# Attention heads' values in the second half of the rounded-token tiles, the samples' rows of w_out multiplied amid attention

## The chip, the cores and the metric

The kernel runs on one core of one Trainium2 chip. The time is the device time of one launch in microseconds, here the median over several executions. The engines of the core are TensorE (PE, with its weight loads counted apart as PEld), VectorE (DVE), ScalarE (ACT), GpSimd (POOL) and SyncE (SP), which issues most of the transfers between the chip's memory and the on-chip buffers.

## The reference

One inference step of a decoder of two layers: a gated-linear-attention layer, then a differential-attention layer, each followed by a squared-ReLU MLP and layer norms. There is one prompt of 1024 tokens (plus 16 meta tokens) and there are 8 running samples with one new token each; a sample's past is 4096 keys and values in a paged cache. What matters here is the second layer's attention and the product with its output matrix `w_out` (1024 x 1024):

```python
def diff_core(q, k, v, q_pos, k_pos, lam):
    s = jnp.einsum('bqhmd,bkhmd->bhmqk', q, k).astype(F32) * (DIFF_DH ** -0.5)
    s = jnp.where(k_pos[None, :] <= q_pos[:, None], s, -jnp.inf)
    p = jax.nn.softmax(s, axis=-1)
    a = p[:, :, 0] - lam * p[:, :, 1]
    return jnp.einsum('bhqk,bkhe->bqhe', a, v.astype(F32))

def diff_output(o, g_sub, lam_init, w_out, dtype):
    o = rms_norm(o, g_sub) * (1.0 - lam_init)
    return o.reshape(B, T, DIFF_HEADS * DIFF_DV).astype(dtype) @ w_out
```

There are 8 heads with keys and queries of 2 x 64 and values of 128 columns. Both the prompt's tokens and the 8 samples go through `diff_output` with the same `w_out`.

## The kernel before

**Products.** Everything is float32. A large product is made of three matmuls on rounded operands (`mm3`, lines 199 to 201): each operand is split into a rounded part "hi" and the rest "lo", and hi x hi, hi x lo and lo x hi are added up in PSUM (tile `mmt`). The tokens' rounded parts are `XH` and `XL`, two tiles each (one for 512 tokens, with room for 8 blocks of features of 516 columns). A weight matrix comes in units of 256 columns (`kunit`, lines 176 to 191): four loads of 256 KB into `raw` (two buffers), four casts on ACT into `whi` (L186), four subtractions on POOL into `wlo` (L187). The tiles `whi` and `wlo` have two buffers each, so two units can be on the chip.

**The stages around the change.** The second layer's projection `w_in` runs with 12 units up to about 1777 us. Then comes the prompt's attention, one head after the other, to about 2051 us; then the product with `w_out` (its first matmuls lie inside the last head, its last at about 2160 us); then the MLP, in which PE is busy throughout.

**Attention.** A head has eight steps of 128 queries. `prep` (L1087, L195, L196) transposes the head's keys and queries, loaded by `load_qk` into `rqk`, and splits them into hi and lo: 1040 + 1024 = 2064 columns in the tile of `XH` and `XL` that belongs to the head's parity. The next head is prepared during this one. `front` makes a step's scores: PE (L1186, tile `prt`), DVE masks and takes the maximum (L1188), ACT takes the exponential (L1190, tile `as`), DVE combines both maps (L1194). `back` transposes that (PE, L1207, tile `axt`), ACT copies it to SBUF (L1209, `aT`), and PE multiplies it with the head's values (L1212) into an accumulator, tile `smt`, which has two buffers during attention; four steps share one accumulator, and ACT reads it twice, for the copy to `Y` (L1262) and the squares (L1266). `load_v` brings the head's values, 512 KB, one head ahead, into a buffer of `whi` which is idle then. When four or eight steps of the last head are done, `o_norm` and `o_fm` (L1232, L1233, L1234) normalise and transpose the tokens into `XH` and `XL` for `w_out`, one block of 128 features after the other.

**w_out.** `w_out` goes through four units and two halves of the tokens: units 0 and 1 with the first half, the same two with the second half, then units 2 and 3. Each unit and half has two accumulators. The generator `samples` is entered after the fourth accumulator: the samples' attention result `oT` is normalised (L1334 to L1340, with a power on POOL, L1339), put into `zoT`, a tile with 32 columns for each of 8 feature blocks, and multiplied with the rows of `w_out` in `s_rows` (L519): 16 matmuls of 32 columns, four on the four column groups of the array for each pair of feature blocks. They read the raw rows of `w_out` again, sixteen loads of 256 KB into five buffers `rw` (L1320). `s_post` (from L522) adds the residual and normalises.

**What sets the order.** The program text gives priorities, and a scheduler that simulates a timeline fixes the order of instructions on each engine at build time. Each engine then takes its instructions in that order and stops at one whose inputs or buffers are not ready. All transfers issued by SP form one such order too.

## Time and profile before

| what | us |
|---|---|
| median of 3 runs | 2855.34 (2853.87 to 2857.34) |
| the profiled execution, its own time | 2854.81 |
| its span, first to last instruction | 2853.1 |
| mean granted TensorE clock | 0.989 of full |
| attention, about | 1778 to 2051 |
| w_out, its first to its last matmul | 2023.8 to 2154.1 |
| samples' 32-column matmuls in it | 2075.6 to 2102.5 |

How to read the rows that the prediction shows. A row of the timeline has start, duration, engine, line, operation, output and inputs with their shapes, a count of records, and in brackets the idle time of the engine before it with what ended it. One 32-column matmul of float32 operands leaves two records, a transpose or a matmul of `mm3` one. Matmuls are pipelined, so the duration of one (0.28 us for w_out's) is longer than the distance to the next. A row of the windows has, for a stretch of time, its length, the busy time of each engine with the number of instructions, the clock, the share of the DMA engines' time and GB/s. A row of waits has the engine, its instruction and the instruction it waited for, with the sum, the number of times and the longest.

### The profile page before, as it was taken

To read this page: it belongs to the slowest core of one execution; us is meant where nothing else is said; L and a number is where in the kernel's file an instruction comes from. 1 tells how busy PE (TensorE), PEld (TensorE's weight loads), DVE (VectorE), ACT (ScalarE), POOL (GpSimd) and SP (SyncE) were. 2 spreads that over 40 slices of the span, in tenths; PEclk is the share of its full clock that TensorE was granted. 3 is DMA by queue.
4 is the path that set the end of the run, shared out by engine and by line. 5 is a ranking of instruction groups with operands and counts; after the bars stand their busy time and mean duration, and the time that the engine had idled before them with its cause. 6 is when DMAs were issued, how large, how long until landed. Compare 5 with 4: busy or idle time off the path is not lost.

```text
span 2853.1 us, 52265 instructions
## 1 busy us (share of the span) xinstructions
PE 2741.4 (96%) x19849; PEld 2241.7 (79%) x19849; DVE 1950.0 (68%) x3046; ACT 1094.0 (38%) x2229; POOL 1112.0 (39%) x744
## 2 busy tenths in 40 slices
PE   8889999999999999999999999998999999999997
PEld 5666677997777777777799988777888889797985
DVE  2565454668888777777667731888538887878788
ACT  3233344242221321221242112777615546355553
POOL 1221212233343443434234321000326767777764
PEclk9899999999999999999999999999999999999998
DMA  7557741634798898988648994111334455554574
GB/s 255 176 174 260 266 171 39 233 103 154 264 338 308 308 353 300 359 293 322 255 161 321 355 375 133 39 53 49 113 105 89 112 129 116 135 123 115 129 190 89
DMA packets 271833, 560.71 MB, mean 197 GB/s; under 512 B 23559, under 2 KB 138829, under 8 KB 267485
## 3 DMA queue, kind: packets, MB, share of 16 engines
q1 hardware_dynamic: 252284, 520.66, 52.2%
q0 software_dynamic: 19296, 36.71, 7.8%
q8 instruction: 156, 2.56, 0.4%
q14 instruction: 97, 0.79, 0.1%
HBM read 531.16 MB, written 29.26 MB: 196 GB/s over the span
## 4 chain that ended last, share of the span: by engine, by line
PE 74%; DVE 8%; DMA 6%; issue 5%; ACT 4%; POOL 2%; SPq 0%; DVEq 0%; POOLq 0%; ACTq 0%
PE mmt L199 18%; PE mmt L200 17%; PE mmt L201 17%; PE smt L843 4%; PE axt L199 3%; PE axt L200 3%; PE axt L201 3%; ACT as L1190 2%; PE smt L1212 2%; PE prt L1186 1%; PE smt L519 1%; DVE pg L802 1%; DMA swt<-in_mlp_w 1%; PE axt L1207 1%; DMA pg<-in_cache_k 1%
## 5 line engine op out<-in xcount | busy, mean ns | idle before, releaser
L187 POOL TENSOR_TENSOR wlo<-raw,whi 128x512 fp32r<-128x512 f32 x256 | 369.4, 1456 | 770.7 <-ACT whi L186 714.7
L199 PE MATMUL mmt<-whi,XH 128*128 128x256 f32 (+1 forms) x1760 | 523.3, 300 | 2.5 <-ACT Y L323 2.0
L200 PE MATMUL mmt<-wlo,XH 128*128 128x256 f32 (+1 forms) x1760 | 524.1, 299 | 1.5 <-POOL wlo L187 1.5
L199 PE MATMUL mmt<-XH,whi 128*128 128x512 f32 (+1 forms) x1216 | 435.2, 358 | 5.0 <-DVE Y L913 3.0
L201 PE MATMUL mmt<-whi,XL 128*128 128x256 f32 x1536 | 435.1, 285 | 0.0
L201 PE MATMUL mmt<-XH,wlo 128*128 128x512 f32 (+1 forms) x1216 | 431.4, 355 | 0.0
L186 ACT CAST whi<-raw 128x512 fp32r<-128x512 f32 x256 | 152.8, 620 | 593.9 <-PE mmt L201 201.4
L803 DVE TENSOR_REDUCE sc<-pg 128x16 f32<-128x1024 f32 x256 | 308.4, 1211 | 71.5 <-POOL pg L802 69.0
L200 PEld LDWEIGHTS mmt<-wlo,XH 128*128 128x128 f32 x1760 | 331.9, 189 | 28.9 <-issue 16.4
L199 PEld LDWEIGHTS mmt<-whi,XH 128*128 128x128 f32 x1760 | 330.2, 189 | 28.5 <-issue 13.5
L200 PE MATMUL mmt<-XL,whi 128*128 128x512 f32 x768 | 306.2, 399 | 0.0
L802 DVE TENSOR_TENSOR pg<-pg,qb 128x1024 f32<-128x1024 f32 x192 | 258.0, 1351 | 63.0 <-DMA pg<-in_cache_k 56.9
L201 PEld LDWEIGHTS mmt<-whi,XL 128*128 128x128 f32 x1536 | 289.3, 189 | 8.8 <-issue 8.0
L199 PEld LDWEIGHTS mmt<-XH,whi 128*128 128x128 f32 x1216 | 229.1, 189 | 52.2 <-issue 12.9
L802 POOL TENSOR_TENSOR pg<-pg,qb 128x1024 f32<-128x1024 f32 x64 | 165.3, 2584 | 260.8 <-DMA pg<-in_cache_k 198.1
L201 PEld LDWEIGHTS mmt<-XH,wlo 128*128 128x128 f32 x1216 | 229.1, 188 | 34.5 <-issue 1.7
L199 PE MATMUL mmt<-whi,HH 128*128 128x512 f32 x512 | 205.4, 402 | 5.0 <-DVE Y L1027 4.7
L201 PE MATMUL mmt<-whi,HL 128*128 128x512 f32 x512 | 204.5, 399 | 0.0
L200 PE MATMUL mmt<-wlo,HH 128*128 128x512 f32 x512 | 204.0, 398 | 0.0
L1441 POOL TENSOR_TENSOR wlo<-RW,whi 128x512 fp32r<-128x512 f32 x96 | 172.3, 1827 | 47.8 <-ACT whi L1440 47.6
L1441 POOL TENSOR_TENSOR wlo<-rw,whi 128x512 fp32r<-128x512 f32 x92 | 157.4, 1747 | 82.3 <-ACT whi L1440 70.1
L200 PEld LDWEIGHTS mmt<-XL,whi 128*128 128x128 f32 x768 | 145.0, 189 | 38.3 <-issue 7.1
(424 smaller groups left out, 5706.2 us busy)
## 6 DMA issues: line engine op xcount, KB each, us to landing
pg<-in_cache_k SPq DMA_DIRECT2D x256, 512.0 KB, 5.8
pg<-in_cache_v SPq DMA_DIRECT2D x256, 512.0 KB, 6.3
raw<-in_mlp_w SPq DMA_DIRECT2D x164, 256.0 KB, 3.7
swt<-in_mlp_w SPq DMA_DIRECT2D x32, 1024.0 KB, 5.1
rw<-in_mlp_w SPq DMA_DIRECT2D x116, 256.0 KB, 3.4
RW<-in_mlp_w POOLq DMA_DIRECT2D x96, 256.0 KB, 5.7
raw<-in_gla_w_in SPq DMA_DIRECT2D x48, 256.0 KB, 3.5
swt<-in_gla_w_in SPq DMA_DIRECT2D x12, 1024.0 KB, 4.9
```

Source lines behind the costliest of these rows:

```text
L186: S.copy(hi[:, c], raw)
L187: G.tensor_tensor(lo[:, c], raw, hi[:, c].bitcast(F32), op=ALU.subtract)
L199: TE.matmul(ps, ah, bh, start=first, stop=False)
L200: TE.matmul(ps, ah, bl, start=False, stop=False)
L201: return TE.matmul(ps, al, bh, start=False, stop=last)
L519: TE.matmul(ps[o : o + TS, :], lhs[:, k + i, :], t[:, i, c * 512 : (c + 1) * 512], start=k == 0, stop=k == nk - 2)
L802: eng.tensor_tensor(pg, pg, qb, op=ALU.mult)
L803: return V.tensor_reduce(sc[:, n, :], pg.rearrange("p (h d) -> p h d", d=64), op=ALU.add, axis=AX.X).ins
L843: m = TE.matmul(acc[i * TS : i * TS + 16, :256], w[r, n, :], pg[r, i * 256 : (i + 1) * 256], start=n == 0, stop=n == NPG).ins
L1190: S.activation(sc_[:, m, :W], sc_[:, m, :W], AF.Exp, bias=mns[:, m : m + 1], scale=-1.0, accum_out=l[:, m : m + 1])
L1212: TE.matmul(out, at, v, start=j == 0, stop=j == t + 1)
L1441: G.tensor_tensor(lo[:, k, :], t, hi[:, k, :].bitcast(F32), op=ALU.subtract)
```

## The change

`XH`'s two tiles become two parts of four feature blocks each. `prep` uses the first part only, whose 4 x 516 columns are just the 2064 that it needs. In attention the memory of the second part (tags XH01 and XH11) is a tile `XA` for each parity of the heads, and the values are loaded there; the buffers of `whi` and `wlo` are then free for the first two units of `w_out`, which are loaded, cast and subtracted from the end of the projection on. The parts are made anew (`xh_part`) after the last head's first half and after attention. In the tile of the even heads there is room left for the samples' operand (columns 1024 to 1280) and their result (1280 to 1792).

The samples' norm stands ahead of the first head. `samples_rows` then loads the rows of `w_out` as eight transfers of 512 KB into two buffers, `sw0` and `sw1`, multiplies them with the samples during five steps of heads 3 and 4 (counted from 0), copies the accumulator to `XA` on ACT and writes it to a scratch `srow` in the chip's memory. In the `w_out` stage `samples` only reads `srow` back and calls `s_post`.

```diff
     def __getitem__(self, at):
         p, k, s = at
         c = s.start // 512
-        return self.t[c][p, k, s.start - 512 * c : s.stop - 512 * c]
+        t = self.t[c]
+        if isinstance(t, list):
+            t, k = t[k // 4], k % 4
+        return t[p, k, s.start - 512 * c : s.stop - 512 * c]
...
-    XH = Halves([cp.tile([P, NB, TH], F32R, name="XH%d" % c, tag="XH%d" % c) for c in range(2)])
+    def xh_part(c, i):
+        return cp.tile([P, 4, TH], F32R, name="XH%d%d" % (c, i), tag="XH%d%d" % (c, i))
+
+    XH = Halves([[xh_part(c, i) for i in range(2)] for c in range(2)])
...
-        xh, xl = (x.t[h % 2].rearrange("p a n -> p (a n)") for x in (XH, XL))
+        xh, xl = (x.rearrange("p a n -> p (a n)") for x in (XH.t[h % 2][0], XL.t[h % 2]))
...
+    xa = [cp.tile([P, 4 * TH], F32, name="XA%d" % c, tag="XH%d1" % c) for c in range(2)]
+
     def load_v(h):
 
         vr = A["v_rows_p"][0, 0, :, h, :]
-        vx = wsp.tile([P, 2048], F32R, name="whi").bitcast(F32)[:, :1024].rearrange("p (t d) -> p t d", d=P)
+        vx = xa[h % 2][:, :1024].rearrange("p (t d) -> p t d", d=P)
...
     open_banks(pr=2, ax=2, sm=2)
+    oq = a1.tile([P, 8, NS], F32, name="zoq")
+    V.tensor_tensor(oq, oT, oT, op=ALU.mult)
+    ps = smt()
+    TE.matmul(ps[:, :64], one, oq.rearrange("p h b -> p (h b)"), start=True, stop=True)
+    V.tensor_scalar(oq.rearrange("p h b -> p (h b)"), ps[:, :64], 1.0 / P, EPS, ALU.mult, ALU.add)
+    G.tensor_tensor(oq, oq, bc(mhalf, [P, 8, NS], 1), op=ALU.pow)
+    V.tensor_tensor(oq, oq, oT, op=ALU.mult)
+
+    def samples_rows():
+
+        wd_ = A["diff_w_out"][0]
+        soT = xa[0][:, 1024:1280].rearrange("p (k t) -> p k t", t=TS)
+        V.memset(soT, 0.0)
+        V.tensor_scalar(soT[:, :, NM : NM + NS], oq, gs, None, ALU.mult)
+
+        def rows(k):
+            t = a1.tile([P, D], F32, name="sw%d" % (k % 2))
+            dma(t, wd_[k * P : (k + 1) * P, :])
+            return t
+
+        ws = [rows(0), rows(1)]
+        yield
+        ps = smt()
+        for k in range(0, NB, 2):
+            for i in range(2):
+                for c in range(2):
+                    o = (2 * i + c) * TS
+                    TE.matmul(ps[o : o + TS, :], soT[:, k + i, :], ws[k + i][:, c * 512 : (c + 1) * 512], start=k == 0, stop=k == NB - 2)
+            if k + 2 < NB:
+                ws += [rows(k + 2), rows(k + 3)]
+                yield
+        sev = xa[0][:, 1280:1792]
+        S.copy(sev, ps)
+        dma(A["srow"], sev)
+        yield
...
+            if h == 3 and n == 7 or h == 4 and n < 4:
+                next(srows)
...
     def samples():
 
-        oq = hp.tile([P, 8, NS], F32, name="zoq")
...
-        s_post(s_rows(soT, A["diff_w_out"][0], NB), 2, hp)
+        sev = s2()
+        dma(sev, A["srow"])
+        s_post(sev, 2, hp)
         yield
```

Line numbers after the change are larger: L1186 becomes L1197, L1207 becomes L1218, L1212 becomes L1223, L1232 becomes L1243, L186 becomes L193, L195 becomes L202 and L1107 becomes L1116.

**Place 1: heads 3 and 4.** On PE, `prt` are scores, `axt` transposes, `smt` products with values. Before, in head 4:

```order
L1087 MATMUL axt<-c_ident,rqk 128x128 x4
L1186 MATMUL prt<-XH_83 128x144 x2
L1186 MATMUL prt<-XL_85,XH_83 128x144 x2
L1186 MATMUL prt<-XH_83,XL_85 128x144 x2
L1207 MATMUL axt<-c_ident,as 128x128 x4
L1186 MATMUL prt<-XH_83 128x336 x2
L1186 MATMUL prt<-XL_85,XH_83 128x336 x2
L1186 MATMUL prt<-XH_83,XL_85 128x336 x2
L1207 MATMUL axt<-c_ident,as 128x128 x5
L1212 MATMUL smt<-vm_21036,aT 128x128
L1212 MATMUL smt<-whi,aT 128x128 x7
```

After, from the same transposes of `rqk` on (`sw_` are the rows of `w_out`, `XA_` the operand of the samples, both in one line):

```order
L1096 MATMUL axt<-c_ident,rqk 128x128 x4
L1197 MATMUL prt<-XH_84 128x144 x2
L1197 MATMUL prt<-XL_88,XH_84 128x144 x2
L1218 MATMUL axt<-c_ident,as 128x128 x4
L1197 MATMUL prt<-XH_84,XL_88 128x144 x2
L1276 MATMUL smt<-sw_22556,XA_21043 32x512 x2
L1197 MATMUL prt<-XH_84 128x336 x2
L1197 MATMUL prt<-XL_88,XH_84 128x336 x2
L1197 MATMUL prt<-XH_84,XL_88 128x336 x2
L1276 MATMUL smt<-sw_22558,XA_21043 32x512 x2
L1218 MATMUL axt<-c_ident,as 128x128 x5
```

Two pairs of samples' matmuls stand between the scores. In all there are eight such places in a row of some fifty: three matmuls, one, and six times two; and the head's first products with its values have moved behind the third load's. SP's order of loads there is now the following, where before no load of `w_out` stood before the last head's values:

```order
L1080 DMA rqk<-out_k_rows_p 128x8x128
L1081 DMA rqk<-qd 128x8x128
L1266 DMA sw_22556<-in_diff_w_out 128x1024
L1079 DMA rkm<-out_k_rows_p 16x128
L1266 DMA sw_22558<-in_diff_w_out 128x1024
L1175 DMA vm_21040<-out_v_rows_p 16x128
L1176 DMA XA_21044<-out_v_rows_p 128x8x128
L1266 DMA sw_22633<-in_diff_w_out 128x1024
L1266 DMA sw_22635<-in_diff_w_out 128x1024
L1266 DMA sw_22680<-in_diff_w_out 128x1024
L1080 DMA rqk<-out_k_rows_p 128x8x128
```

A `sw_` load waits at SP for the matmuls of the load two before it; head 5's values and keys stand behind.

**Place 2: the end of the last head.** On PE, between two groups of transposes of finished tokens (`axt<-c_ident,Y`), matmuls of `w_out` on the feature blocks that are there. Before:

```order
L1232 MATMUL axt<-c_ident,Y 128x128 x4
L201 MATMUL mmt<-whi,XL_85 128x256
L199 MATMUL mmt<-whi,XH_83 128x256
L200 MATMUL mmt<-wlo,XH_83 128x256
L201 MATMUL mmt<-whi,XL_85 128x256
L199 MATMUL mmt<-whi,XH_83 128x256
L1232 MATMUL axt<-c_ident,Y 128x128 x4
```

After:

```order
L1243 MATMUL axt<-c_ident,Y 128x128 x4
L208 MATMUL mmt<-whi,XL_88 128x256
L206 MATMUL mmt<-whi,XH_84 128x256
L207 MATMUL mmt<-wlo,XH_84 128x256
L208 MATMUL mmt<-whi,XL_88 128x256
L206 MATMUL mmt<-whi,XH_84 128x256
L207 MATMUL mmt<-wlo,XH_84 128x256
L208 MATMUL mmt<-whi,XL_88 128x256
L206 MATMUL mmt<-whi,XH_84 128x256
L207 MATMUL mmt<-wlo,XH_84 128x256
L1243 MATMUL axt<-c_ident,Y 128x128 x4
```

Where there were 5 to 7 matmuls between groups there are 9: the third accumulator is unit 1's.

**Place 3: the end of the projection.** On ACT, `qo` are the projection's results, the casts into `XH_` the keys of the first two heads, `as` the exponentials. Before:

```order
L195 CAST XH_83<-axt 128x512 x4
L1107 COPY qo<-mmt 128x512 x2
L195 CAST XH_84<-axt 128x16
L195 CAST XH_84<-axt 128x512
L1190 ACTIVATE as,ls<-as,ast 128x1040 x2
```

After:

```order
L202 CAST XH_84<-axt 128x512 x4
L1116 COPY qo<-mmt 128x512 x2
L193 CAST whi<-raw 128x512 x2
L202 CAST XH_86<-axt 128x16
L202 CAST XH_86<-axt 128x512
L1201 ACTIVATE as,ls<-as,ast 128x1040 x2
```

Two casts of `w_out`'s unit 1 stand ahead of the second head's keys; unit 0's four stand before the last projection results, and unit 1's other two between the first head's exponentials.

More of the change, by code (lines that the diff above doesn't have):

```diff
@@ L159, in hybrid_step @@
     A["qd"] = dr.tile([T, D], F32, name="qd")
+    A["srow"] = dr.tile([P, 512], F32, name="srow")
     ident = cload("ident")
@@ L522, in s_post @@
     def s_post(ps, ln, pool):
-        sev = s2()
-        V.tensor_copy(sev, ps)
+        sev = ps
+        if pool is spool:
+            sev = s2()
+            V.tensor_copy(sev, ps)
         pt = smt()
@@ L1267, in hybrid_step @@
         if n == 3 and h == 7:
+            XH.t[0][1] = xh_part(0, 1)
             o_norm(slice(0, 4), slice(7, 8))
@@ L1275, in hybrid_step @@
     o_norm(slice(4, 8), slice(7, 8))
+    XH.t[1][1] = xh_part(1, 1)
     for j in range(8):
@@ L1332, in samples @@
     def samples():
-        oq = hp.tile([P, 8, NS], F32, name="zoq")
-        V.tensor_tensor(oq, oT, oT, op=ALU.mult)
-        ps = smt()
-        TE.matmul(ps[:, :64], one, oq.rearrange("p h b -> p (h b)"), start=True, stop=True)
-        V.tensor_scalar(oq.rearrange("p h b -> p (h b)"), ps[:, :64], 1.0 / P, EPS, ALU.mult, ALU.add)
-        G.tensor_tensor(oq, oq, bc(mhalf, [P, 8, NS], 1), op=ALU.pow)
-        V.tensor_tensor(oq, oq, oT, op=ALU.mult)
-        soT = hp.tile([P, NB, TS], F32, name="zoT")
-        V.memset(soT, 0.0)
-        V.tensor_scalar(soT[:, :, NM : NM + NS], oq, gs, None, ALU.mult)
-        s_post(s_rows(soT, A["diff_w_out"][0], NB), 2, hp)
+        sev = s2()
+        dma(sev, A["srow"])
+        s_post(sev, 2, hp)
         yield
@@ L1401, in chip_operand @@
     def chip_operand(terms, quarter, n, tmp):
-        buf = XH.t[count[0] % 2].rearrange("p k n -> p (k n)")
+        parts = [x.rearrange("p k n -> p (k n)")[:, : 4 * n] for x in XH.t[count[0] % 2]]
         count[0] += 1
-        parts = [buf[:, i * 4 * TH : i * 4 * TH + 4 * n] for i in range(2)]
         hi, lo = (x.rearrange("p (k n) -> p k n", n=n) for x in parts)
```

1 line of the change is left out of this document (added).

## The prediction

> **What bounds the kernel now.** I read the page's busy shares and the chain of waits first, then the windows over attention and the second layer's w_out, then TensorE's waits and the timeline in the places that the change touches. The page and its chain:
>
> ```profile
> PE 2741.4 (96%) x19849; PEld 2241.7 (79%) x19849; DVE 1950.0 (68%) x3046; ACT 1094.0 (38%) x2229; POOL 1112.0 (39%) x744
> PE 74%; DVE 8%; DMA 6%; issue 5%; ACT 4%; POOL 2%; SPq 0%; DVEq 0%; POOLq 0%; ACTq 0%
> ```
>
> TensorE (PE) bounds the whole, but the average hides where it does not. The windows give, after the stretch in us and its length, the busy us of PE, its weight loads, VectorE (DVE), ScalarE (ACT) and GpSimd (POOL), the granted clock, the DMA share and GB/s:
>
> ```profile
> 1904.00:1939.00 35.00, 31.25 (x244) 25.86 (x244) 27.42 (x93) 25.41 (x77) 2.90 (x1) 0.95 0.18 47
> 1925.00:1930.00 5.00, 3.20 (x24) 2.07 (x25) 4.96 (x11) 3.23 (x7) 0.00 (x0) 1.00 0.53 140
> 1930.00:1934.00 4.00, 4.00 (x22) 3.83 (x23) 2.29 (x9) 2.48 (x7) 0.00 (x0) 0.58 0.38 91
> 2020.00:2031.00 11.00, 6.66 (x56) 5.82 (x53) 10.90 (x27) 8.03 (x22) 1.14 (x2) 1.00 0.47 158
> 2031.00:2051.00 20.00, 19.43 (x170) 19.11 (x169) 3.57 (x5) 7.34 (x14) 0.00 (x0) 1.00 0.08 28
> 2051.00:2065.00 14.00, 13.62 (x112) 13.22 (x113) 6.72 (x14) 7.72 (x19) 10.94 (x6) 1.00 0.83 257
> 2065.00:2092.00 27.00, 26.47 (x174) 19.30 (x172) 6.04 (x11) 2.38 (x4) 14.60 (x9) 1.00 0.71 203
> 2092.00:2112.00 20.00, 20.00 (x128) 14.80 (x128) 7.43 (x15) 2.38 (x4) 4.47 (x5) 1.00 0.21 70
> ```
>
> Head 4 (first row) leaves PE 3.75 us idle; in 1925 to 1930 DVE is the one that is full (4.96 of 5). Head 7's end (2020 to 2031) is DVE's too: 10.90 of 11, PE idle 4.34. From 2031 on PE is full, so a PE instruction taken out there shortens the program by what it occupied, and one put into attention costs only what the idle time does not take.
>
> **1. The samples' rows leave w_out.** What the sixteen 32-column matmuls (L519) cost there, by the timeline and by the windows of their tile (zoT) and of w_out's own (mmt), the last one undisturbed:
>
> ```profile
> 2075.65 1.90 PE L519 MATMUL smt<-rw,zoT 128*32 128x512 f32 x10
> 2083.50 0.28 PE L199 MATMUL mmt<-whi,XH 128*128 128x256 f32 x1
> 2083.71 1.05 PE L519 MATMUL smt<-rw,zoT 128*32 128x512 f32 x2
> 2084.69 0.39 PE L200 MATMUL mmt<-wlo,XH 128*128 128x256 f32 x1
> 2084.91 0.28 PE L201 MATMUL mmt<-whi,XL 128*128 128x256 f32 x1
> 2075.43:2102.45 27.02, 13.34 (x32) 1.89 (x32) 0.00 (x0) 1.00 0.57 171
> 2075.43:2102.45 27.02, 14.69 (x100) 12.24 (x99) 1.38 (x2) 0.00 (x0) 1.00 0.57 171
> 2112.00:2124.00 12.00, 12.00 (x102) 11.85 (x102) 1.37 (x2) 0.00 (x0) 1.00 0.47 155
> ```
>
> A matmul of w_out takes 12.00/102 = 0.118 us when nothing comes between. In the 27.02 us stand 100 of them, 11.8 us; the other 15.2 us belong to the samples, in twelve places: a group of five (two records each) and eleven single ones. All of it goes: **-15.2**. From 2083.50 to 2084.91 are 1.41 us with one single and two steps of 0.118 in them: a single one occupies 1.17. Four on four different column groups cost no more than one:
>
> ```profile
> 38.51 1.07 PE L351 MATMUL smt<-swt,sx 128*32 128x512 f32 x8
> ```
>
> **2. They come back in heads 3 and 4.** The new order has them in eight places, one of three, one of one, six of two, where two of one load use two column groups. At 1.17 a place that is 8 x 1.17 = 9.4 us of PE work, among these waits:
>
> ```profile
> PE axt L1207 <- DVE XL L196: 2.8, 3, 1.8
> PE smt L1212 <- ACT aT L1209: 1.9, 3, 0.8
> 1918.78 0.66 PE L1207 MATMUL axt<-c_ident,as 128*128 128x128 f32 x4 [0.76 <-DVE XL L196]
> 1919.85 0.33 PE L1207 MATMUL axt<-c_ident,as 128*128 128x128 f32 x1 [0.41 <-ACT aT L1209]
> 1928.54 0.66 PE L1207 MATMUL axt<-c_ident,as 128*128 128x128 f32 x4 [1.80 <-DVE XL L196]
> ```
>
> Beside the three waits (2.97) there is the clock: 4.00 us at 0.58 are 4.00 x 0.42 = 1.7 us more than at full clock, and PE work in the gap ahead of it may keep it up. I take 4.7 as absorbed. The trace has no PE gap over 1.80 us here and still shows 0.58. [...] The row decides that the dip is there; whether filling cures it no trace here shows.
>
> The rows come as eight loads of 512 KB into two buffers, so each of the last six is issued when the load two before has been multiplied. The nearest row for one is a key load in head 4; the slowest of that size is a page of the cache on busy queues:
>
> ```profile
> rqk<-out_k_rows_p SPq DMA_DIRECT2D x1, 512.0 KB, 4.2
> pg<-in_cache_v SPq DMA_DIRECT2D x256, 512.0 KB, 6.3
> ```
>
> Between release and use the order has about 4 to 8 us of PE work, least for the third and the fifth load (some 4.0 to 4.7 by the durations of those rows). I take 0.8 for both together, from 4.2; at 6.3 six loads could cost up to 6 x 1.5 = 9. SP holds the next head's values and keys behind a waiting load, but these are used a head later. The accumulator occupies one of two PSUM buffers (tile smt), so head 4's first value product waits for head 3's last squares; the order moved it behind transposes, and I price it at nothing, hidden by those. Sum: 9.4 - 4.7 + 0.8 = **+5.5**, bounds 0 (all of it in the head's 3.75 idle, with the clock and the load wait) and +14 (nothing absorbed, half of the 9).
>
> **3. w_out's first two units are ready when head 7 ends.** Their values no longer take a whi buffer, so loads, four ACT casts and four POOL subtractions per unit move from here to before attention. In head 7 stand unit 0's casts, then unit 1 arrives late:
>
> ```profile
> PE axt L1232 <- DVE XL L1234: 4.6, 4, 2.2
> 2010.00 0.62 ACT L186 CAST whi<-raw 128x512 fp32r<-128x512 f32 x1
> 2016.09 0.62 ACT L186 CAST whi<-raw 128x512 fp32r<-128x512 f32 x1
> 2051.11 0.65 PE L1232 MATMUL axt<-c_ident,Y 128*128 128x128 f32 x4 [0.68 <-DVE XL L1234]
> 2057.57 0.39 PE L200 MATMUL mmt<-wlo,XH 128*128 128x256 f32 x1 [0.20 <-POOL wlo L187]
> ```
>
> Between two blocks of four transposes (L1232; a feature block of the tokens) PE had two accumulators to feed, both of unit 0, 6 matmuls = 0.7 us a block; now unit 1's first makes three, 9 = 1.06 us. Six blocks come late, 6 x 0.36 = 2.1 of the 4.34 idle between 2020 and 2031. The 0.68 at 2051 and the 0.20 at 2057, which waits for unit 1, go too: **-3.0**, bounds 0 and -4.9 (all of 4.34 and half of the rest). What is multiplied in the gaps no longer stands in the full stretch behind them.
>
> **4. At attention's start** the order puts unit 1's first two casts, which need the projection's last buffer, ahead of the second head's key cast on ACT, and six small zoq instructions on DVE, PE and POOL:
>
> ```profile
> 1777.57 0.59 ACT L1107 COPY qo<-mmt 128x512 f32<-128x512 f32 x1 [5.11 <-PE mmt L201]
> 1778.05 0.81 ACT L195 CAST XH<-axt 128x16 fp32r<-128x16 f32 x2
> 1782.00 1.17 ACT L1190 ACTIVATE as<-as,ast 128x1040 f32<-128x1040 f32 x1 [3.14 <-DVE ast L1188]
> 2060.38 10.55 POOL L1339 TENSOR_TENSOR zoq<-zoq,mhalf 128x64 f32<-128x64 f32 x1 [1.60 <-DVE zoq L1338]
> ```
>
> Two casts at 0.52 are 1.0 before the key cast, and DVE's score pass stands behind the subtraction that follows it; with 0.5 for the zoq pieces **+1.5**, bounds 0 (ACT's 3.14 idle hides it) and 2. The 10.55 of POOL runs beside attention, where POOL is nearly empty; nothing needs its result for two heads.
>
> **5. Unit 2 comes earlier.** Its third and fourth raw loads go out only after unit 0's whi is free and ACT has cast the first two:
>
> ```profile
> 2079.84 1.14 ACT L186 CAST whi<-raw 128x512 fp32r<-128x512 f32 x2 [14.99 <-DMA rw<-in_diff_w_out]
> 2090.15 0.62 ACT L186 CAST whi<-raw 128x512 fp32r<-128x512 f32 x1 [2.47 <-DMA raw<-in_diff_w_out]
> raw<-in_diff_w_out SPq DMA_DIRECT2D x12, 256.0 KB, 3.6
> ```
>
> Cast 1.14, load 3.6, cast 0.62, a POOL subtraction of 1.3 to 1.8 and the handovers make 7.5 to 8.8 us; PE has 73 matmuls of unit 1 before it (8.6) and 12 more before it needs the third piece (1.4), 10.0 in all. Zero, bounds 0 and +1. The samples' loads, which before pushed the fourth cast to 2090.15, are gone from this queue.
>
> **Sum:** -15.2 + 5.5 - 3.0 + 1.5 = -11.2 on the profiled run's 2854.81 (span 2853.1), which lies 0.5 under the median 2855.34: **2844.1**. From unit 2 on the order of PE is as before, so the gain carries to the end.
>
> **The rivals.**
> A. *Attention absorbs nothing.* The row of 1925 to 1930 speaks for it: DVE is full and set the pace, and if PE work delays DVE's inputs, the clock still dips. Then 9.4 + 0.8 and 2.0 at the start: -15.2 + 10.2 - 3.0 + 2.0 = -6.0, 2849.3; with 2 to 3 us for slower loads 2852. Against it: PE idles in just those places.
> B. *The two buffers stall PE, slower.* PE takes its work in order, so a sample matmul that waits for its load holds the scores and transposes behind it, and DVE and ACT run dry. It decides from where the six reloads wait together over 15.2 + 3.0 - 9.4 - 1.5 = 7.3 us (1.2 each). With 6.3 us loads, 2.1 each over 4.2, and a lost lead of as much again for the refill: 6 x 4 = 24, +16.7: 2872. Against it: DMA share 0.18 in head 4, so loads should land in 4.2.
> C. *More is absorbed.* Attention +1, the tail -4.9, and ACT, 20.97 busy of 23 us before 2023, also gives back unit 0's four casts (2.1): with nothing at the start -15.2 + 1 - 4.9 - 1 = -20, 2835.
> D. *The early weights bring nothing.* DVE holds 2020 to 2031 at 10.90 of 11 whatever PE has; if the extra matmuls only delay the transposes DVE waits for, the -3.0 is lost: -8.2, 2847.1.
>
> **How the numbers follow.** Forecast 0.50, A 0.20, B 0.09, C 0.10, D 0.11. About 0.2% (5.7 us) is what a measurement of this kernel tells from no change, so faster is below 2849.6, slower above 2861. Faster: 0.48 of the forecast, C, D with 0.10, half of A: 0.78. Same: half of A and the rest, 0.13. Slower: B, 0.09. The forecast's own range is 2838 to 2849; to hold 8 in 10 the range takes in A's upper part and most of C: 2836 to 2854.
>
> **What would show it.** Step 1: no 32-column matmuls in the second w_out, and its 768 matmuls at 0.118 without breaks. Step 2: heads 3 and 4 together 5.5 longer, the 1.80 wait gone and the clock above 0.58 there; waits on the sample rows' loads under 1 us (over 7.3 in sum: rival B). Step 3: PE idle between the first w_out matmul and its full stretch near 1 us. Step 4: the first long exponential 1 to 2 us later after the projection's last matmul. Step 5: no wait of unit 2's first matmuls on POOL or ACT. I am wrong if head 4 grows by its whole 9.4, or if the tail's idle moves to another place behind it.

## The result, and the profile after

| | before | after |
|---|---|---|
| median of 11 runs each, us | 2857.41 (2853.57 to 2864.35) | 2847.01 (2842.84 to 2854.69) |
| ratio, 95% interval | | 0.9962 (0.9952 to 0.9973), -10.4 us |
| the profiled execution, its own time | 2854.81 | 2854.69 |
| its span | 2853.1 | 2852.8 |

The kernel became faster by 10.4 us; 2844.1 was predicted. The two profiled executions are equally long all the same: that of after is the longest of its 11, that of before, 2854.81, lies 2.6 below the median of its 11. So the two profiles may not be compared by their ends. They are compared here by stages, and the first table holds all fourteen traces of this study. A head begins with its first exponential of 1040 columns on ACT, the attention with the projection's last copy of `qo`, and the MLP with w_out's last matmul; each number is the distance of two such rows of the timeline, in us. (w_out's last matmul stands at 2154.1 in before; the "about 2160" of the description ahead is too late.)

| kernel | start and head 0 | head 2 | head 4 | head 6 to first w_out matmul | w_out, first to last | projection's end to w_out's end | MLP |
|---|---|---|---|---|---|---|---|
| before | 33.5 | 33.7 | 35.3 | 56.2 | 130.3 | 376.5 | 699.0 |
| before again (e9) | 32.8 | 33.7 | 35.3 | 56.6 | 129.8 | 375.5 | 697.7 |
| before, third (e12) | 32.7 | 33.7 | 35.3 | 56.4 | 130.6 | 376.1 | 705.2 |
| tiles split only (e11) | 32.9 | 33.7 | 35.4 | 56.6 | 129.8 | 375.7 | 704.1 |
| after | 35.6 | 33.7 | 40.1 | 55.4 | 112.7 | 364.9 | 706.9 |
| after again (e7) | 35.6 | 35.1 | 40.4 | 55.4 | 112.5 | 366.4 | 702.7 |
| weights only (e1) | 36.3 | 33.7 | 35.4 | 54.1 | 127.5 | 374.3 | 704.3 |
| samples only (e2) | 34.1 | 35.2 | 40.1 | 58.1 | 114.5 | 369.4 | 706.4 |
| fours, one buffer (e3) | 35.4 | 35.1 | 36.3 | 55.4 | 112.4 | 362.6 | 703.7 |
| the same again (e10) | 35.7 | 33.7 | 36.1 | 55.6 | 112.4 | 361.5 | 705.4 |
| unit 1 later (e4) | 33.4 | 32.6 | 41.1 | 54.6 | 112.5 | 363.2 | 703.0 |
| fours, unit 1 mid head 2 (e5) | 33.5 | 35.5 | 35.5 | 56.7 | 113.7 | 365.7 | 703.8 |
| samples twice (e6) | 34.8 | 35.1 | 45.5 | 55.6 | 113.7 | 372.1 | 706.5 |
| fours, unit 1 later (e8) | 33.2 | 32.6 | 36.1 | 56.6 | 113.7 | 361.8 | 704.9 |

Heads 1, 3 and 5 are not in the table. They take 29.7, 28.8 to 28.9 and 28.8 to 28.9 in every trace but these: head 1 takes 31.3 in e4 and e8, head 3 takes 32.3 in e5, head 5 takes 29.5 in e3, e8 and e10.

Up to w_out's end the change is worth 11.7 us by the first profile of each (376.5 and 364.9 are rounded), where 11.2 was forecast. In the second trace of the change, e7, it is 1.5 less: its head 2 has a stretch at half clock and takes 35.1 for 33.7. Then the MLP of the profiled execution is 7.9 longer, and the projection ended 3.5 later (1781.03 against 1777.57), where of the change only the split tiles and unit 0's loads and casts are there; over all fourteen traces it ends between 1772.4 and 1785.3.

The page of after, its busy shares and its chain of waits:

```profile
PE 2741.8 (96%) x19849; PEld 2247.6 (79%) x19849; DVE 1962.4 (69%) x3045; ACT 1095.6 (38%) x2230; POOL 1104.5 (39%) x744
PE 72%; DVE 10%; DMA 7%; issue 4%; ACT 4%; POOL 2%; SPq 0%; DVEq 0%; POOLq 0%; ACTq 0%
```

PE has as many matmuls as before and bounds the whole as before; neither line tells that 11 us were won. The windows do, by the columns of the prediction's: head 4, head 7's end from the first w_out matmul on, its full stretch, and w_out where the samples' matmuls used to stand.

```profile
1909.00:1949.00 40.00, 37.94 (x279) 25.77 (x278) 27.62 (x93) 26.29 (x78) 2.90 (x1) 1.00 0.40 126
2029.00:2040.00 11.00, 9.25 (x74) 7.73 (x71) 10.96 (x31) 9.05 (x25) 1.01 (x1) 1.00 0.31 97
2040.00:2062.00 22.00, 22.00 (x194) 22.00 (x193) 4.48 (x7) 6.26 (x12) 0.00 (x0) 1.00 0.15 49
2080.00:2112.00 32.00, 32.00 (x272) 31.80 (x271) 12.00 (x23) 6.01 (x11) 14.15 (x12) 1.00 0.60 159
```

In the last row PE does 272 matmuls in 32.00 us, 0.118 each and without a break. In head 7's end PE is busy 9.25 of 11 where it was 6.66, with DVE as full as before (10.96). In head 4 it is busy 37.94 of 40 at a clock of 1.00, where it was 31.25 of 35 at 0.95. The eight places are 8.4 us of new work (8 x 1.05); the stretch at half clock, whose price was 1.7, is gone, so PE's busy time grew by 6.69, and with 1.7 less idle (3.75 before, 2.06 now) the two stretches are only 5.0 apart, the heads by the table 4.8. Four rows of PE's timeline show the new matmuls of after (the place of three, the single one, and two of the six places of two; a matmul leaves two records), and its waits from 1900 to 1970 what stands between:

```profile
1918.62 1.06 PE L1276 MATMUL smt<-sw,XA 128*32 128x512 f32 x6
1920.41 1.04 PE L1276 MATMUL smt<-sw,XA 128*32 128x512 f32 x2
1930.58 1.05 PE L1276 MATMUL smt<-sw,XA 128*32 128x512 f32 x4 [0.70 <-DMA sw<-in_diff_w_out]
1942.19 1.05 PE L1276 MATMUL smt<-sw,XA 128*32 128x512 f32 x4
```

```profile
PE smt L1223 <- ACT aT L1220: 1.8, 3, 0.8
PE smt L1276 <- DMA sw<-in_diff_w_out: 0.7, 1, 0.7
PE axt L1218 <- DVE XL L203: 0.2, 1, 0.2
```

The waits of 1.80 and 0.76 for XL are gone and one of 0.2 is left, and one load in eight came late, by 0.70. The waits for aT are as before (1.8 for 1.9).

The end of attention, by PE's waits from 2005 to 2066. The 4.6 us in four waits of the last transposes (L1232 before, L1243 now) for XL are one of 0.2:

```profile
PE mmt L206 <- DVE ast L1199: 0.9, 2, 0.6
PE prt L1197 <- DVE ast L1199: 0.5, 1, 0.5
PE axt L1243 <- DVE XL L1245: 0.2, 1, 0.2
```

The start of attention, ACT's timeline. Two casts of unit 1 (L193) now stand between the last copy and the key casts, and the first long exponential comes 5.71 us after that copy instead of 4.43. The other two stand between the first head's exponentials; the second fence has the last of them, which waits for its load, and the exponential behind it:

```profile
1781.03 0.58 ACT L1116 COPY qo<-mmt 128x512 f32<-128x512 f32 x1 [5.11 <-PE mmt L208]
1781.51 1.14 ACT L193 CAST whi<-raw 128x512 fp32r<-128x512 f32 x2
1782.55 0.66 ACT L202 CAST XH<-axt 128x16 fp32r<-128x16 f32 x2
1786.74 1.17 ACT L1201 ACTIVATE as<-as,ast 128x1040 f32<-128x1040 f32 x1 [3.53 <-DVE ast L1199]
```

```profile
1799.02 0.62 ACT L193 CAST whi<-raw 128x512 fp32r<-128x512 f32 x1 [1.95 <-DMA raw<-in_diff_w_out]
1799.54 0.73 ACT L1201 ACTIVATE as<-as,ast 128x528 f32<-128x528 f32 x1
```

The MLP, by PE's waits from 2500 to 2560 of after. The same stretch of before (2508 to 2568) has no wait of PE that the profile lists:

```profile
PE axt L208 <- POOL wlo L1484: 1.6, 1, 1.6
PE mmt L206 <- DVE HF L1525: 1.2, 1, 1.2
```

Where these come from, on DVE, ACT and POOL of after, one fence with rows of the three timelines:

```profile
2507.30 7.18 DVE L1459 TENSOR_TENSOR RX<-XR,RX 128x1032 f32<-128x1032 f32 x1
2514.86 0.64 ACT L1513 ACTIVATE HF<-HF 128x516 f32<-128x516 f32 x1 [5.76 <-DVE HF L1524]
2507.12 4.10 POOL L1484 TENSOR_TENSOR wlo<-RW,whi 128x512 fp32r<-128x512 f32 x3
2522.33 6.29 POOL L1484 TENSOR_TENSOR wlo<-RW,whi 128x512 fp32r<-128x512 f32 x3 [6.31 <-ACT whi L1483]
```

One subtraction on DVE, 361 us behind w_out's end, takes 7.18 us. ACT then sits idle 5.76 for the DVE work queued behind it, POOL 6.31 for ACT's casts of the weights, and PE waits for POOL and DVE. In before the same instruction takes 2.00 and the three subtractions on POOL beside it 2.10 each:

```profile
2511.97 2.00 DVE L1416 TENSOR_TENSOR RX<-XR,RX 128x1032 f32<-128x1032 f32 x1
2511.05 6.30 POOL L1441 TENSOR_TENSOR wlo<-RW,whi 128x512 fp32r<-128x512 f32 x3
```

The order of instructions on all four engines is the same in both MLPs. The rest of the 7.9 is the clock. The first 110 us behind w_out's end, in before and then in after:

```profile
2154.00:2264.00 110.00, 103.86 (x784) 97.64 (x783) 88.42 (x113) 69.31 (x128) 74.80 (x58) 1.00 0.47 102
```

```profile
2146.00:2256.00 110.00, 103.61 (x765) 98.36 (x764) 84.58 (x109) 66.20 (x124) 71.67 (x56) 0.95 0.45 96
```

PE's waits in there are alike (3.0 and 2.5 before, 3.0 and 2.9 after), but behind them the clock fell in the one execution and not in the other: 110 x 0.05 = 5.5 us. Whether the change does this, or the execution that the profiler happened to take, only further traces can tell.

### The profile page after: what moved, and what is told of

Read it like the earlier page. It is cut to its first block, busy times and chain, and to the rows that moved or that the text cites. A ratio compares the mean times of both kernels' runs of the same rounds, so it can differ in the third digit from the quotient of the medians.

```text
span 2852.8 us, 52251 instructions
## 1 busy us (share of the span) xinstructions
PE 2741.8 (96%) x19849; PEld 2247.6 (79%) x19849; DVE 1962.4 (69%) x3045; ACT 1095.6 (38%) x2230; POOL 1104.5 (39%) x744
## 4 chain that ended last, share of the span: by engine, by line
PE 72%; DVE 10%; DMA 7%; issue 4%; ACT 4%; POOL 2%; SPq 0%; DVEq 0%; POOLq 0%; ACTq 0%
PE mmt L206 17%; PE mmt L207 17%; PE mmt L208 17%; PE smt L852 4%; PE axt L206 3%; PE axt L207 3%; PE axt L208 3%; PE smt L1223 2%; ACT as L1201 1%; DMA swt<-in_mlp_w 1%; PE prt L1197 1%; DVE Y L1555 1%; DVE RX L1459 1%; DMA rw<-in_mlp_w 1%; DMA pg<-in_cache_k 1%
## 5 line engine op out<-in xcount | busy, mean ns | idle before, releaser
L193 ACT CAST whi<-raw 128x512 fp32r<-128x512 f32 x256 | 152.8, 619 | 570.6 <-PE mmt L208 186.6
L811 DVE TENSOR_TENSOR pg<-pg,qb 128x1024 f32<-128x1024 f32 x192 | 266.3, 1394 | 59.4 <-DMA pg<-in_cache_k 51.7
```

The source lines that it names most:

```text
L193: S.copy(hi[:, c], raw)
L811: eng.tensor_tensor(pg, pg, qb, op=ALU.mult)
```

## The experiments

**One half each.** e1 keeps the early weights and puts the samples back into w_out:

```diff
-            if h == 3 and n == 7 or h == 4 and n < 4:
-                next(srows)
...
-        dma(sev, A["srow"])
+        V.tensor_copy(sev, s_rows(soT, A["diff_w_out"][0], NB))
```

> The samples' rows stand in the w_out stage again, as in the kernel before; the values stay in XA and w_out's units 0 and 1 stay early. My theory (the parts add up): from the projection's last copy to the first exponential 5.7 us as in the change (before 4.4), head 4 back to 35.3, from the first to the last w_out matmul 130.3 - 2.4 = 127.9. From the projection's last copy to the last w_out matmul 376.5 (before) + 2.1 - 3.3 = 375.3, so next to nothing is gained: about 2856. Rival (the tail's gain comes from the samples' loads and matmuls leaving the queue, not from the early weights): the stretch of w_out stays at 130.3 and the whole is 2 us longer than before, 378.6.

e2 keeps the samples in attention and gives the values their `whi` buffer back:

```diff
-        vx = xa[h % 2][:, :1024].rearrange("p (t d) -> p t d", d=P)
+        vx = wsp.tile([P, 2048], F32R, name="whi").bitcast(F32)[:, :1024].rearrange("p (t d) -> p t d", d=P)
```

> The samples' rows stay amid attention; the values go into a whi buffer again, so w_out's units are not early. My theory: start 4.4 as before (and perhaps 0.2 for the norm), head 4 +4.8 over before (40.1), first to last w_out matmul 130.3 - 15.2 = 115.1. From the projection's last copy to the last w_out matmul 376.5 - 15.2 + 4.8 = 366.1, against 364.9 of the change. Rival (unit 2 or unit 1 comes too late once the samples do not fill the time, so the early weights are what makes the move pay): w_out 120 or more with waits on POOL or ACT, the whole 371 or more.

The trace's rows for w_out's hi x hi matmuls, with the start of the first and of the last, first of e1, then of e2:

```profile
L206 PE MATMUL mmt<-whi,XH x256: 274/281/388, 2032.1 to 2159.4; 128*128 128x256 f32 x128
```

```profile
L206 PE MATMUL mmt<-whi,XH x256: 274/281/388, 2035.9 to 2150.1; 128*128 128x256 f32 x128
```

To the last matmul of all it is 127.5 in e1 and 114.5 in e2, against 130.3 before and 112.7 with both. So the samples' departure alone is worth 15.8, the early weights alone 2.8 inside w_out and 2.1 ahead of its first matmul (54.1 for 56.2). e2 has no gain ahead of it: 58.1, with a dip of the clock in it. The two halves nearly add up (18.6 for 17.6 inside w_out). Both missed their expected totals. e2 has 369.4 where 366.1 was expected: its head 2 (35.2 for 33.7) and its head 6's end (58.1 for 56.2), each with a stretch at half clock, make up the difference. e1 has 374.3 for 375.3, and its first long exponential comes 7.76 us after the copy where 5.7 was expected. One time each, on a chip on which the kernel before took 2865.03: e1 2865.70, e2 2858.59. The samples carry the gain; e1 loses at attention's start (36.3 for 33.5) more than half of the 4.9 that it wins at the end. Its order at the start is not the change's, though: all four casts of unit 1 stand ahead of the first exponential, and ACT waits 4.33 for a load of theirs, so what the change pays there is read from e4 and not from e1.

**Is it the place or the matmul that head 4 pays for?** e3 loads two feature blocks at once, 1 MB into one buffer, so that four matmuls on four column groups stand together:

```diff
-            t = a1.tile([P, D], F32, name="sw%d" % (k % 2))
-            dma(t, wd_[k * P : (k + 1) * P, :])
+            t = a1.tile([P, 2, D], F32, name="sw%d" % (k // 2 % 1))
+            dma(t, wd_[k * P : (k + 2) * P, :].rearrange("(i p) n -> p i n", p=P))
...
-                ws += [rows(k + 2), rows(k + 3)]
+                ws.append(rows(k + 2))
```

> As the change, but the rows come as four loads of 1 MB into one buffer and are multiplied four at a time: five places (three, one, four, four, four) in place of eight. My theory (head 4 pays for the number of places, each near 1.1 us, less the idle time): 3 x 1.1 = 3.3 us less in head 4, 36.8 in place of 40.1, with perhaps 1 to 2 us back for waits on the one buffer (a 1 MB load takes 5 us). Rival (head 4 pays for the loads' round trips and the accumulator that holds one of two buffers): 40 or more, since the round trips get longer and nothing else changes.

PE's timeline of e3, all rows of these matmuls:

```profile
1922.29 1.06 PE L1276 MATMUL smt<-sw,XA 128*32 128x512 f32 x6
1924.08 1.04 PE L1276 MATMUL smt<-sw,XA 128*32 128x512 f32 x2
1930.19 1.06 PE L1276 MATMUL smt<-sw,XA 128*32 128x512 f32 x8 [1.00 <-DMA sw<-in_diff_w_out]
1938.37 1.06 PE L1276 MATMUL smt<-sw,XA 128*32 128x512 f32 x8
1947.46 1.06 PE L1276 MATMUL smt<-sw,XA 128*32 128x512 f32 x8
```

Five places instead of eight, the same sixteen matmuls (x8 is four of them), and 1.04 to 1.06 whether one, three or four stand there: head 4 takes 36.3 instead of 40.1 and 40.4, 0.9 more than before (head 5 takes 0.6 more). So the number of places counts, not of matmuls. The loads changed with the places, four for eight; e6 leaves them alone. e3's one time is 2851.61.

e6 runs each of these matmuls twice, to see whether PE time in head 4 is paid at all:

```diff
-                    TE.matmul(ps[o : o + TS, :], soT[:, k + i, :], ws[k + i][:, c * 512 : (c + 1) * 512], start=k == 0, stop=k == NB - 2)
+                    for r in range(2):
+                        TE.matmul(ps[o : o + TS, :], soT[:, k + i, :], ws[k + i][:, c * 512 : (c + 1) * 512], start=k + r == 0, stop=k + r == NB - 1)
```

> Each of the sixteen samples' matmuls amid attention is done twice into the same accumulator, so the samples' product with w_out comes out doubled. Loads, places and buffers stay. My theory (PE's time in head 4 is used up, more of it shows at full price): a second pass on the same column groups costs some 0.85 us a place, 8 x 0.85 = 6.8, so head 4 goes from 40.1 to 46 to 47. Rival (head 4's 4.8 come from loads and buffers, and PE still has idle time to give): 40 to 42.

Two of the eight places in the timeline of e6 (its order has the single matmul ahead of the three):

```profile
1922.91 1.92 PE L1277 MATMUL smt<-sw,XA 128*32 128x512 f32 x8
1926.00 1.92 PE L1277 MATMUL smt<-sw,XA 128*32 128x512 f32 x8
```

A doubled place lasts 1.92 for 1.06, eight of them 6.9 more; head 4 grew from 40.1 and 40.4 to 45.5, by 5.3. Of the other 1.6, 1.3 lie in the idle time that the first round had left: it is 2.06 us in after and 0.79 in e6, where PE is busy 44.71 of 45.50. Of the first round's 8.4 us 4.8 to 5.1 were paid, of the second's 6.9 us 5.3: the first round takes most of what head 4 absorbs. So PE's time is what head 4 pays for; the loads are the same in both. e6's one time is 2856.86.

**What the start costs.** e4 holds unit 1 of w_out back until head 1, so that its casts leave the place ahead of the key casts:

```diff
-                units[u] = kunit(w, u * 256)
+                with tc.issue_after(hold[0]) if scaled and u == 1 else nullcontext():
+                    units[u] = kunit(w, u * 256)
...
+    hold.append(exps[16 * 1])
```

> As the change, but w_out's unit 1 is held back to the first step of head 1, so its first two casts no longer stand ahead of the second head's keys. My theory (the casts delay the start): projection's last copy to first exponential 4.6 in place of 5.7 (the norm's small piece stays), first and second head's starts apart 29.1 in place of 29.9, up to 1 us back in head 1 where the four casts now stand; the tail as in the change (112.7). Rival (the start is late because of the norm's instructions on DVE and POOL): 5.3 or more, nothing gained.

ACT's timeline of e4 at the start:

```profile
1777.70 0.59 ACT L1119 COPY qo<-mmt 128x512 f32<-128x512 f32 x1 [5.11 <-PE mmt L208]
1778.18 0.18 ACT L202 CAST XH<-axt 128x16 fp32r<-128x16 f32 x1
1782.30 1.16 ACT L1206 ACTIVATE as<-as,ast 128x1040 f32<-128x1040 f32 x1 [3.14 <-DVE ast L1204]
```

The start is back at 4.60 with ACT's 3.14 idle as in before, and start and head 0 take 33.4 instead of 35.6: unit 1's early casts were worth 2.2 of the 2.6 that these 33 us are longer than in the four traces of the old order (33.0 on average). The other 0.4 stay, no more than those four traces differ (32.7 to 33.5). e5 and e8, which hold unit 1 back too, have 33.5 and 33.2.

Where the 2.2 come from the two timelines show, each counted from the projection's last copy. The first exponential of 1040 columns is 1.1 later in after than in e4 (5.71 and 4.60), the one of 784 columns 1.05 (12.91 and 11.86), the one of 528 columns 2.24 (18.51 and 16.27), and so it stays to the next head. So two casts ahead of the key casts cost their own length, 1.1, and the rest comes between the exponentials, where ACT waits 1.95 for the load of unit 1's last piece. In e6 this wait is 1.07, and start and head 0 take 34.8 for 35.6. The clock does not separate them: over this stage it is 0.86 in after and 0.85 in e4. The exponential of 528 columns in e4:

```profile
1793.97 0.73 ACT L1206 ACTIVATE as<-as,ast 128x528 f32<-128x528 f32 x1 [1.80 <-DVE ast L1204]
```

But unit 1's work then lies further on, and head 1 takes 31.3 for 29.7, of which head 2 gives 1.1 back (32.6 for 33.7). One run took 2845.69.

**Both together.** e5 and e8 have the fours of e3 and hold unit 1 back, e5 to the middle of head 2 (there the scheduler's order has four places of four matmuls each), e8 to head 1. e10 is e3 once more with its time, e7 the changed kernel and e9 the kernel before, for second traces.

```diff
-    hold.append(exps[16 * 1])
+    hold.append(exps[43])
```

> Both together: four loads of 1 MB, now multiplied in exactly four places of four, and unit 1 held back to the middle of head 2. My theory (PE pays per place): head 4 within 1 us of its length before (35.3 with a stretch at half clock, 33.9 without one), start 4.6, first to last w_out matmul 112.5; from the projection's last copy to the last w_out matmul about 360 against 364.9 of the change and 376.5 before, so some 15 us faster than before, ratio 0.9945. Rival (the loads' round trips set head 4): head 4 stays at 38 or more and the ratio at that of the change, 0.996.

> The four-at-a-time rows of e3_quads1, whose places stay (three, one, four, four, four), and unit 1 held back to the first step of head 1 as in e4_unit1_later. My theory (both effects add): start 4.6, heads 0 to 2 together 1 us less than in e3_quads1, head 4 36.3, first matmul of w_out after head 6's start 54 to 55.4; from the projection's last copy to w_out's last matmul 360.5 to 361.5, 4 us less than the change, 15 less than before: ratio about 0.9945. Rival (as in e5_quads_later the new order loses elsewhere what it gains): 364 to 366 and the ratio of the change, 0.996.

> e3_quads1 once more, timed. My theory: 362 to 363 from the projection's last copy to w_out's last matmul, head 4 36.3, ratio 0.995. Rival: head 4's gain was of one execution; 38 or more.

> The changed kernel once more, for a second trace. My theory on its profiled run (3 us waits stand in the MLP in both kernels, and whether the clock is halved behind them differs from run to run): projection's last copy to last w_out matmul 363 to 367 again, the MLP's length not the same as in its first trace (706.9 from w_out's last matmul to the end, 699.0 before) but 699 to 704. Rival (the change itself makes the MLP longer): 705 to 708 again.

> The kernel before once more, for a second trace. My theory (the MLP's length differs from run to run and not by the change): 376 to 378 from the projection's last copy to w_out's last matmul, head 4 35.3 with a stretch at half clock, and 702 to 706 from there to the end, as in the changed kernel's runs, in place of 699.0. Rival (the change lengthens the MLP by 4 to 8 us): 699 again.

| kernel | median, us | before on the same chip | ratio, 95% interval |
|---|---|---|---|
| e7, the change again | 2845.97 (8 runs) | 2859.24 (14 runs) | 0.9955 (0.9937 to 0.9973) |
| e5 | 2843.53 (7) | 2859.24 (14) | 0.9949 (0.9929 to 0.9969) |
| e8 | 2845.12 (6) | 2856.96 (17) | 0.9956 (0.9940 to 0.9973) |
| e10 | 2844.11 (12) | 2856.96 (17) | 0.9955 (0.9940 to 0.9970) |

By stages e10 and e8 are some 3 to 5 us better than the change up to w_out's end (361.5 and 361.8 against 364.9 and 366.4); the intervals, some 4 to 6 us to each side, can't tell any of the four from the others. None is shown to beat the change. e5 missed its 360 by stages (365.7). Its head 4 is as short as expected, 35.5, but heads 3 and 4 together take 67.8, against 69.0 in after, 65.2 in e3 and 64.2 in before, and it has further stretches at half clock; why its head 3 is 3.4 longer was not tested. e9 is the second trace of before: its MLP is 697.7, where 702 to 706 was expected, so at that point the rival, by which the change lengthens the MLP, had its number.

**Does the change lengthen the MLP?** By then all ten traces with the change or one half of it had an MLP of 702.7 to 706.9, the two of before 699.0 and 697.7. Common to all ten is the split of `XH`, so e11 is the kernel before with that alone (the first three pieces of the change above, and one of the same kind in the MLP's product). No instruction moves on any engine; only addresses differ:

```diff
-    XH = Halves([cp.tile([P, NB, TH], F32R, name="XH%d" % c, tag="XH%d" % c) for c in range(2)])
+    XH = Halves([[xh_part(c, i) for i in range(2)] for c in range(2)])
```

> The kernel before with one thing of the change only: XH's two tiles are split into two parts of four blocks each. Values stay in whi, the samples stay in w_out, and the order of all five engines is the same as before. Theory 1 (the split as such, that is where the tiles lie, lets the MLP's long VectorE instructions fall beside GpSimd's): the RX instruction some 357 us behind w_out's last matmul takes about 7.5 us in place of 1.2 to 2.0, and the MLP, from w_out's last matmul to the end, takes 703 to 706 us in place of 698 to 699; the time comes out 4 to 7 us above the kernel before. Theory 2 (it hangs on when w_out ends, since the MLP's weights are loaded at another time against its products): RX at 1.2 to 2.0 us and the MLP at 697 to 700, as before; time equal to before within 2 us. Theory 3 (nothing but the choice of executions: before's two profiles were among its fastest): the MLP may come out anywhere from 698 to 706 here, and in the third profile of before too, while the times agree within 2 us.

> The kernel before, unchanged, for a third profile on the same chip. Theories 1 and 2: the MLP at 697 to 700 us and the RX instruction at 1.2 to 2.0 us once more. Theory 3: the MLP at 702 to 706 with a long RX instruction, as in the changed kernels.

e11 took 2859.52 (10 runs) beside 2860.39 for the kernel before (13 runs), ratio 0.9996 (0.9980 to 1.0012): the split costs nothing. Its profiled MLP took 704.1, but for another reason: the DVE instruction in question is short, and a dip of the clock behind two waits for XH lies some 14 us ahead of it. PE's waits, windows and DVE's timeline of e11:

```profile
PE axt L206 <- DVE XH L202: 2.8, 2, 1.9
```

```profile
2496.00:2500.00 4.00, 2.12 (x12) 1.91 (x11) 4.00 (x5) 1.61 (x4) 3.87 (x3) 0.68 0.36 114
2500.00:2504.00 4.00, 4.00 (x20) 4.00 (x20) 4.00 (x4) 0.75 (x2) 3.65 (x3) 0.50 0.43 133
```

```profile
2513.92 2.00 DVE L1421 TENSOR_TENSOR RX<-XR,RX 128x1032 f32<-128x1032 f32 x1
```

e12 is the kernel before, unchanged, and has everything that after has. Its rows of DVE and POOL, and PE's waits from 2500 to 2570:

```profile
2514.48 7.23 DVE L1416 TENSOR_TENSOR RX<-XR,RX 128x1032 f32<-128x1032 f32 x1
2514.34 4.11 POOL L1441 TENSOR_TENSOR wlo<-RW,whi 128x512 fp32r<-128x512 f32 x3
```

```profile
PE axt L201 <- POOL wlo L1441: 1.6, 1, 1.6
PE mmt L199 <- DVE HF L1482: 1.2, 1, 1.2
```

The same two waits to the tenth, the same long instruction, and the clock at 0.97 in the first 110 us behind w_out: an MLP of 705.2 without any change. So the long MLP comes without the change too. That the change makes it more frequent stays possible: the instruction was long in ten of ten traces of the changed kernels, in one of four of the old order, and three short ones drawn by chance out of the fourteen would all fall among those four in 4 of 364 cases. The mean MLPs lie 704.8 - 701.5 = 3.3 apart. Taken whole, that would leave about 10.3 - 3.3 = 7.0 of the gain, while the first comparison has 7.7 to 13.7 in its interval and the second 7.7 to 18; so the whole of it is hardly the change's. These runs settle no more.

## Why the prediction was right

The forecast was -11.2 on 2855.34. The medians give -10.4 and, on another chip, -13.3 (e7), the stages up to w_out's end -11.7 and, between the means of the four traces of the old order (376.0) and of the two of the change (365.7), -10.3. The time itself, 2847.01, is 2.9 above the forecast; 2.1 of that is the base, since the eleven runs of before have a median of 2857.41.

1. **The samples leave w_out, -15.2:** 15.8 by e2, 15.3 against e9. The term held, and so did 0.118 for a matmul of w_out.
2. **They come back, +5.5:** 4.8 in after and 5.1 in e7, in head 4. A place came to 1.05 and not to 1.17, so 8.4 for 9.4; the waits absorbed less than the 3.0 (PE's idle time fell by 1.7, the 0.70 for the late load included), and the clock gave its 1.7. The mechanism is the predicted one: the wait of 1.80 is gone, the clock stays at 1.00, one load is late by 0.70 (0.8 was the term), and eight places are paid by the place (e3) and nearly in full beyond the idle (e6). That the dip goes with the gap, left open in the prediction, is so in eight of the nine traces with the samples in these heads; e5 has a clock of 0.59 from 1927 to 1931. The dip was there in all four traces of the old order and in e1, the five in which the gap is left (lowest clock of a window of 4 us there: 0.58 in before, 0.68 in e9, 0.77 in e11, 0.75 in e12 and in e1).
3. **The early weights, -3.0:** 0.9 ahead of w_out's first matmul and 2.4 inside it in after (17.6 less term 1's 15.2), 3.3; without a dip of the clock (e1) 2.1 and 2.8, 4.9, which is the bound of the term (4.34 and half of 0.88 make 4.8, not 4.9). So the term was too small, and what it gave beyond 3.0 went to a dip at head 6's end that no term of the sum has (0.50 over 3.41 us in after): it stands there in eight of the nine traces with the samples in attention (not in e4) and in none of the other five. The section on the hardware has its rows. PE's idle time in the eleven us around the first w_out matmuls went from 4.34 to 1.75, not quite to the 1 that was forecast.
4. **The start, +1.5, bounds 0 and 2:** too small. 2.1 against the first profile, 2.6 against the mean of the old order. The casts cost 2.2 (e4), not 1.0. The two that the prediction priced held, with 1.1. The other two of unit 1, between the first head's exponentials, it put at nothing; there ACT waits 1.95 for a load, and the lag grows from 1.05 to 2.24.
5. **Unit 2, 0:** no wait of PE in w_out from 2066 to its end.

So the sum is close in part by luck: the weights were worth more than was forecast, the start cost more, and a dip that was not forecast took back some of the weights' gain.

**"So the gain carries to the end"** is the step that the two equally long profiled executions seemed to refute, and the medians and e12 restored. What it left out is that the stage behind has waits of its own that differ by 7 to 8 us from one execution to the next, and that the sum was set on an execution with a short MLP.

The rivals fall by the same rows. A (attention absorbs nothing) needed 9.4 in head 4, B 7.3 us of load waits for 0.7, C +1 in attention, and D the loss of the 3 us of early weights. D's time, 2847.1, is almost the measured one all the same; only the stages refute it (PE busy 9.25 of 11 for 6.66 at head 7's end, and the 4.9 of e1).

## What to carry to other kernels

A small product on a full engine was cheapest here where the engine idles for others, but only as far as the idle goes (of the first round's 8.4 us in head 4 4.8 to 5.1 were paid, of the second's 6.9 us 5.3); behind it each place cost nearly its whole length, however few of the column groups it uses (1.04 to 1.06 us with one to four matmuls), so fewer and fuller places cost less there (head 4: 36.3 for 40.1; the medians do not yet tell them apart). Compare two profiles by the stages that the change touches, and look at a second and third trace of the old kernel before a change in a stage behind is explained. When work is moved ahead of a stage, price all of it, with the loads it waits for: two casts ahead of the first step cost their own length (1.1 us), and a third and fourth among its exponentials as much again, because one waited for its load in front of them (1.95 us).

## What the runs showed of the hardware

**Clock.** The clock fell to half behind PE gaps of 1.8 to 3.0 us, and behind the same gaps it fell in one execution and not in another: behind the 3.0 and 2.5 to 2.9 us at the MLP's beginning it lost 5.5 us in after (0.95 over 110 us) and nothing in before (1.00). The windows show where the drops lie. In before and after the stretches at half clock begin on a grid of 3.41 us (in before at 1783.18, 1800.25 and 1929.95, 5 and 38 slots apart) and, up to the last 20 us, last 3.41 us or a multiple of it; the rows below set beside them how much of PE's idle time falls into one slot of the grid. At head 6's end PE waits 1.47 and 0.32 us close together in before and in after alike. Two slots of after, then two of before:

```profile
1999.84:2003.25 3.41, 1.62 (x14) 0.94 (x11) 3.41 (x9) 2.30 (x6) 0.00 (x0) 1.00 0.00 0
2003.25:2006.66 3.41, 3.41 (x16) 2.73 (x15) 2.64 (x9) 2.40 (x6) 0.00 (x0) 0.50 0.02 5
```

```profile
1987.99:1991.40 3.41, 2.44 (x20) 1.76 (x19) 3.41 (x11) 2.27 (x6) 0.69 (x1) 1.00 0.00 0
1991.40:1994.81 3.41, 2.59 (x18) 1.83 (x19) 3.37 (x8) 1.47 (x3) 0.00 (x0) 1.00 0.82 286
```

In after both waits lie in one slot, PE is busy for 1.62 of its 3.41 us, and the next slot runs at 0.50. In before the border of two slots cuts through them, PE is busy for 2.44 and 2.59, and the clock stays. Head 4's wait of 1.80 in before lies in one slot (1926.57 to 1929.98, PE busy 1.61); at the MLP's beginning the slots with the waits have 1.37 and 1.16 in after (from 2150.02 and 2197.80 on; half clock follows both), and 1.80 and 1.73 in before (from 2158.65 and 2206.44 on; it follows neither). In before and after, from 450 to 2815 us, every slot at full clock with PE busy for less than 1.65 us is followed by half clock and none with more than 2.1; between them both occur (before has a drop behind 2.06, from 1796.84 on, and none behind 1.69, from 2022.12 on).

**DVE beside POOL.** A subtraction of two inputs on DVE, 1.23 us in the trace e9, takes 7.18 us in after, 7.23 in e12 and 7.54 in e10, where the first of three subtractions on POOL begins 0.18 and 0.14 us ahead of it and 0.17 behind; those three then run at 1.37 each. A fourth follows, and DVE's ends 1.1 us after the fourth (after: POOL's ends at 2513.38, DVE's at 2514.48). Where POOL began 0.9 us ahead (before, e11), DVE's took 2.00 and POOL's 2.10 each; where POOL began 0.54 behind (e9), 1.23 and 2.11. So over 6 us on DVE lie between a POOL that begins 0.17 behind and one that begins 0.54 behind, and in after and e12 two waits of PE, 1.6 and 1.2, come with the long one.

In before POOL's first subtraction, of 1.82, ends 0.90 into DVE's, which is done 1.10 later. In e10 DVE's record begins 0.17 us ahead of POOL's first and ends behind POOL's fourth all the same. What holds DVE there no run shows.
